# Score products of two attentions: a 64-row operand becomes a zero-padded 128-row one

## The chip, the cores and the metric

The kernel runs on one core of one Trainium2 chip. The metric is the device time of one execution in microseconds (us); several runs are taken and their median is compared. Engines are named as the profile names them: PE is TensorE's matmul, PEld its weight load, DVE VectorE, ACT ScalarE, POOL GpSimd, SP SyncE.

## The reference, cut to what matters

Two layers of a transformer over 256 context and 256 latent tokens: a feed-forward half step, a token mixer, a second feed-forward half step, and a last norm. The token mixer runs three branches (an mLSTM scan, differential attention, neighbourhood attention), gates them and merges them through `w_branch` and `w_out`. The change concerns the scores of the two attentions, which have heads of 64 features:

```python
    # differential attention: 4 heads, each with two score maps
    s1 = (jnp.einsum('bhqd,bhkd->bhqk', q1, k1) * scale).astype(jnp.float32)
    s2 = (jnp.einsum('bhqd,bhkd->bhqk', q2, k2) * scale).astype(jnp.float32)
    p = jax.nn.softmax(s1, axis=-1) - lam * jax.nn.softmax(s2, axis=-1)
...
    # neighbourhood attention: 8 heads; latent keys carry a bias, context keys none
    s_lat = (jnp.einsum('bnqhd,bknwhd->bnhqkw', qb, kb) * scale).astype(jnp.float32) + bias
    s_ctx = (jnp.einsum('bnqhd,bchd->bnhqc', qb, kc) * scale).astype(jnp.float32)
```

In the first layer context queries (which see context keys alone) are worked out too; in the last layer only latent queries.

## The kernel before, in words

**Arithmetic.** Matrices are multiplied in float32 by splitting each number into a part with its leading 11 bits (`hi`) and the rest (`lo`), and adding up hi x hi, hi x lo and lo x hi. `three` (L228) issues these three products for one block of 128 x 128 weights against all tokens of a slice (512 columns in the first layer, 256 or 512 in the last); `dense` (L234) runs `three` over the blocks and calls `tick` after each. Weights are loaded by SP into a ring `raw`, split into `whi` on ACT (L217) and `wlo` on DVE (L218).

**Scores.** `halves` (L905) takes a projection with two heads of 64 features on the 128 partitions (in PSUM) and builds tiles of 128 rows. For queries, tile j holds head j's leading part on its own 64 partitions and its rest on the other 64. For keys, tile j holds head j's leading part twice; one further tile `rest` holds the rest of both heads, each on its own 64 partitions. `qk_scores` (L918) then issues two products per head and query tile of 128: L920 multiplies the queries' leading part with the keys' rest, over the head's own 64 rows; L921 multiplies the whole query tile with the doubled keys, over all 128 rows. The query tile is the operand that is loaded as weights, the keys (512 columns, or 256 for context queries) stream. Both add up in one PSUM bank.

```python
            own = slice(64 * j, 64 * j + 64)
            mm(pS[:, 0:nk], q[j][own, bb], k[2][own, 0:nk], start=True, stop=False)
            mm(pS[:, 0:nk], q[j][:, bb], k[j][:, 0:nk], start=False, stop=True)
```

**Who calls it.** `df_head` (L954) and `na_pair` (L1032) each work on two heads (j = 0 and 1) per query tile, so four score products come in a row. Each is a generator of three stages per query tile, run by `piped` (L943): `scores` (products, then maximum on DVE, exponential on ACT, normalising on DVE), `turned` (transposes on PE at L652, copied out by ACT) and `read` (products with the values, L991 and L1073). There are four calls of `df_head` and four of `na_pair` in each of two layers. `df_qk` (L933) and `na_qk` (L1024) make the tiles for the next one.

**Order of work.** PE's order is the program's order; the tile framework orders the other engines by priority and sets all semaphores. The dense products of `merge` (gates, the next head's projections, the branch product) run as the main stream, and `Beside` lets a generator make a step after given ticks: `spread` with the lists `AT_FULL` (first layer) and `AT_LAT` (last). So the score products of one head stand between dense products of other work.

**Buffers.** Nearly all tiles of the mixer of 128 x 512 words come from one ring with the tag `t2k` of `TB` = 17 places: gate vectors, convolutions, decay weights, query and key tiles, exponentials, transposed exponentials, biases. `mt2` (L767), read by the mLSTM heads at L833, has a room of its own. POOL does few things here: a power in `pow_rstd` (L646), the loads of the neighbourhood bias (`na_bias`, L1017) which it issues itself, and small memsets.

Of the kernel before, what the change touches and what calls it, by code (L numbers as in the profile page):

```python
# [10 lines left out]
F32 = mybir.dt.float32  # L11
F32R = mybir.dt.float32r
# [4 lines left out]
P = 128  # L17
# [7 lines left out]
T = NCTX + NLAT  # L25
# [10 lines left out]
TB = 17  # L36
# [18 lines left out]
class Beside:  # L55
    """Work for the gaps of a stream of dense products: steps of generators, spread over its ticks."""
# [7 lines left out]
    def at(self, gen, ticks):  # L64
        """Steps of a generator after that many ticks from now."""
        self.timed.append([gen, [self.count + t for t in ticks]])
# [25 lines left out]
class Joined:  # L92
    """[P, n, T] in two tiles, the second from the place m: its room serves another tile before."""
# [18 lines left out]
def tile_backbone(ctx: ExitStack, tc: tile.TileContext, I, out: bass.AP):  # L112
# [36 lines left out]
    # silu(c), in 32 columns of which the first two are tokens  # L149
# [7 lines left out]
    def ada_first(l, mod, part, room):  # L157
        """Half of one of the nine vectors, as products, a step per 256 rows of w_ada."""
        pa = psum()
        c0 = mod * D + part * 512  # L160
        for k2 in range(KC // 2):
            raw = room[:, k2, :]
            nc.sync.dma_start(out=raw.rearrange("p (k c) -> p k c", k=2),
                              in_=I["w_ada0"][k2 * 256:(k2 + 1) * 256, c0:c0 + 512].rearrange("(k p) c -> p k c", k=2))
            for k in range(2):
                kc = 2 * k2 + k
                for j in range(4):
                    mm(pa[32 * j:32 * j + 32, 0:P], sc[:, kc, :], raw[:, k * 512 + j * P:k * 512 + (j + 1) * P],
                       start=kc == 0, stop=kc == KC - 1)
            yield  # L170
        rows = np_.tile([P, 256], F32, tag="rows", name="rows", bufs=1)[:, 0:P]
        with tc.high_priority(offset=AHEAD):
            nc.scalar.copy(rows, pa[:, 0:P])
        yield
        pt = psum()
        nc.tensor.transpose(pt[:, 0:P], rows, ident)
        ks = slice(4 * part, 4 * part + 4)
        v = pt[:, 0:P].rearrange("p (j c) -> p j c", j=4)
        with tc.high_priority(offset=AHEAD):
            for cls in range(2):  # L180
                nc.vector.tensor_tensor(modT[l][:, mod, cls, ks], v[:, :, cls], b_ada[:, l, mod, ks], ALU.add)
                if mod % 3 == 1:
                    nc.vector.scalar_tensor_tensor(amod[l][:, mod // 3, cls, ks], modT[l][:, mod, cls, ks], 1.0,
                                                   norm_g[:, l, mod // 3, ks], ALU.add, ALU.mult)

    def ada(l, mod, pool, scb, junk):
        """One of the nine vectors beside dense products: 64 columns of w_ada on each half of the
        partitions, of one half of its rows each, times silu(c) and added up along the rows."""
        acc = pool.tile([P, KC, 2, 2], F32, tag="acc", name="acc", bufs=2)
        for kc in range(KC):  # L190
            raw = wp.tile([P, 1024], F32, tag="raw", name="raw", bufs=4)
            nc.sync.dma_start(out=raw, in_=I["w_adaT"][l, mod, kc])
            for i in range(2):
                w = raw[:, i * 512:(i + 1) * 512]
                for cls in range(2):
                    nc.vector.scalar_tensor_tensor(w if cls else junk, w, 1.0, scb[:, cls, :], ALU.mult, ALU.mult,  # L196
                                                   accum_out=acc[:, kc, i, cls:cls + 1])
            yield
        other = pool.tile([P, KC, 2], F32, tag="other", name="other", bufs=2)
        for i in range(2):  # L200
            own, far = slice(64 * i, 64 * i + 64), slice(64 - 64 * i, 128 - 64 * i)
            nc.scalar.copy(other[own], acc[far, :, i, :])
            nc.vector.tensor_tensor(other[own], other[own], acc[own, :, i, :], ALU.add)
        for cls in range(2):
            nc.vector.tensor_tensor(modT[l][:, mod, cls, :], other[:, :, cls], b_ada[:, l, mod, :], ALU.add)
        which, what = divmod(mod, 3)
        if what == 1:
            for cls in range(2):
                nc.vector.scalar_tensor_tensor(amod[l][:, which, cls, :], modT[l][:, mod, cls, :], 1.0,
                                               norm_g[:, l, which, :], ALU.add, ALU.mult)  # L210
        elif what == 2:
            nc.vector.tensor_scalar_mul(gmod[l][:, which], modT[l][:, mod], 0.5 if which == 1 else 0.25)
        yield

    def split(hi, lo, src):
        """The leading 11 bits of float32 numbers, and the rest."""
# [11 lines left out]
    def three(dst, w, wat, a, aat, start, stop):  # L228
        """dst (+)= w.T @ a in float32, of parts with 11 bits: the weights stay."""
# [4 lines left out]
    def dense(pt, w, k0, a, at, first, last, n=KC):  # L234
        """n blocks of 128 rows of the weights, the k0-th of the product first."""
# [19 lines left out]
    def rstd_cols(cs):  # L255
        """1 / rms of the tokens of cs, on partitions, a column per 128 of them."""
# [10 lines left out]
    def rstd_rows(cs):  # L267
        """1 / rms of the tokens of cs, on every partition, in PSUM."""
# [21 lines left out]
    def norm_mod(l, which, h, cls):  # L290
        """h of one class of tokens; steps with a wait between them."""
# [18 lines left out]
    def norm_begin(l, which, h, before):  # L310
        """h of the context tokens, beside the last products of the sub-layer in front, which are
        of latent tokens; then the steps that lead to h of those."""
# [18 lines left out]
    def load_late():  # L331
        """Constants that later parts read: behind the first weights."""
# [38 lines left out]
    def ffn(l, i, classes, out_classes_next, before, vectors):  # L371
        """`before` is the end of the sub-layer in front: its last products of latent tokens."""
# [28 lines left out]
        def cold_start(n):  # L401
            """The first n units of the kernel. Shift and scale of its first norm come in halves."""
# [47 lines left out]
        def warm_start():  # L450
            """The first pair of tiles, of the scaled x alone, while the rest of the norm is worked out:
            1 / rms multiplies their products, and the products of the shift are added."""
# [20 lines left out]
            # the row 32 * g for g, a part of a unit of weights  # L473
# [25 lines left out]
        elif both:  # L499
            # two pairs of tiles take the context first, while the norm of the latent tokens runs  # L500
# [40 lines left out]
        def whole(dt):  # L541
# [5 lines left out]
            if not both:  # L547
                # what the last norm takes, with its weights, in the place of the context tokens
# [34 lines left out]
    def mixers(l, before):  # L583
# [64 lines left out]
        def transposed(tiles):  # L648
            """Blocks [128, 128] side by side, each transposed, in PSUM."""
# [55 lines left out]
        # -- mLSTM: gates and values --  # L705
# [61 lines left out]
        mt2 = mp.tile([P, T], F32R, name="mt2")  # L767
# [8 lines left out]
        # [token, tile, (g fwd, g bwd, m fwd, m bwd), head]  # L776
# [31 lines left out]
        # query tiles that a key tile reaches, per direction  # L808
# [92 lines left out]
        # -- differential attention --  # L901
# [3 lines left out]
        def halves(pt, cs, key):  # L905
            """Two heads of 64 features in parts of 11 bits, one tile of 128 rows per head: of
            queries both parts, of keys the leading part twice; and the rest of the keys."""
            two = [t2r("st") for _ in range(2)]
            rest = t2r("rest") if key else None
            for j, t in enumerate(two):  # L910
                own, other = slice(64 * j, 64 * j + 64), slice(64 - 64 * j, 128 - 64 * j)
                nc.scalar.copy(t[own, cs], pt[own, cs])
                if key:
                    nc.scalar.copy(t[other, cs], pt[own, cs])
                nc.vector.tensor_sub((rest[own, cs] if key else t[other, cs]), pt[own, cs], t[own, cs].bitcast(F32))
            return two + [rest] if key else two

        def qk_scores(pS, q, k, j, bb, nk):  # L918
            own = slice(64 * j, 64 * j + 64)
            mm(pS[:, 0:nk], q[j][own, bb], k[2][own, 0:nk], start=True, stop=False)  # L920
            mm(pS[:, 0:nk], q[j][:, bb], k[j][:, 0:nk], start=False, stop=True)  # L921

        def rope(pt):
            """Latent tokens of a projection turned, in place."""
# [18 lines left out]
        def piped(stages, items):  # L943
            """Item n is in stage s at step n + s; a wait after every piece."""
# [61 lines left out]
        # -- neighbourhood attention --  # L1006
        relb = I["relb"]

        def na_bias(b, hp2):
            """8 * bias + mask of two heads for the query tile b: [query, head, key row, key column]."""  # L1010
# [72 lines left out]
        # -- the order of work: products, with the attention of the head in front beside them --  # L1083
# [60 lines left out]
        def ended(dt, pt):  # L1144
            for cls in (0, 1) if full else (1,):
                residual(l, 1, dt, pt, cls, True)
            if not full:
                # what the next norm scales, without 1 / rms, in the place of the context tokens
# [39 lines left out]
    # the last norm: tokens to partitions while 1 / rms is worked out  # L1188
# [52 lines left out]
def _layout(i):  # L1241
    """Arrays as the chip reads them: moved, padded with zeros, never computed with."""
# [18 lines left out]
    def blocks(w, n):  # L1261
        """[.., K, n * 128] -> [.., n, 128, K]: per column block, its rows' 128 x 128 blocks side by side."""
# [61 lines left out]
```

## Time and profile before

| | us |
|---|---|
| median of 3 runs | 2328.62 |
| lowest and highest | 2328.49, 2329.36 |
| span of the profiled execution, first to last instruction | 2327.4 |
| PE busy (share of the span) | 2294.7 (99%) |
| DVE busy | 1583.6 (68%) |
| ACT busy | 936.7 (40%) |
| POOL busy | 63.3 (3%) |

The page gives the profiled execution by its span; the median of the runs is 1.2 us longer, which is what lies around the span. PE's busy share is the share of time in which some product is between its start and its modelled end; since products are pipelined, the distance from one start to the next tells more than the duration of one.

### The profile page before, as it was taken

The page shows a single profiled execution, that of the slowest core. Times are in us where ns is not written, and L with a number is a line of the kernel's source. Part 1 is how long each engine was busy: PE and PEld are TensorE (multiplying, and loading weights), DVE is VectorE, ACT ScalarE, POOL GpSimd, SP SyncE. Part 2 cuts the span into 40 slices and gives each one's busy share as a digit, 9 for nine tenths or more (in the row PEclk, how much of TensorE's full clock was granted, in tenths as well). Part 3 has the DMA queues.
Part 4 walks back from the last instruction along what each step waited for, and adds up shares of the span by engine and source line. Part 5 has one row for each costly group of instructions (what it writes and reads, how often), then busy time and mean ns, then how long its engine had stood idle before and what let it go on. Part 6 is the DMA issues. An engine that isn't in the chain of part 4 may idle for free.

```text
span 2327.4 us, 33611 instructions
## 1 busy us (share of the span) xinstructions
PE 2294.7 (99%) x12877; PEld 1952.4 (84%) x12877; DVE 1583.6 (68%) x3394; ACT 936.7 (40%) x1683; POOL 63.3 (3%) x101
## 2 busy tenths in 40 slices
PE   7999999999999999999999999999999999999998
PEld 5888889888777777888888898888898988899998
DVE  5989934786665553676666569998347875768654
ACT  4332222455544443333322233322234665555443
POOL 0000000000001100000000000000000001100000
PEclk9999999999999999999999999999999999999999
DMA  8555633212123322334444436555333233445554
GB/s 297 181 199 199 206 114 97 102 61 73 65 74 88 82 77 77 109 109 158 150 161 141 141 103 206 206 202 192 92 96 109 89 121 115 121 140 170 185 179 134
DMA packets 94257, 315.54 MB, mean 136 GB/s; under 512 B 13152, under 2 KB 13936, under 8 KB 94096
## 3 DMA queue, kind: packets, MB, share of 16 engines
q1 hardware_dynamic: 89072, 308.07, 39.1%
q0 software_dynamic: 2144, 4.36, 1.4%
q8 instruction: 101, 1.65, 0.3%
q10 hardware_dynamic: 2880, 0.96, 0.2%
q14 instruction: 60, 0.49, 0.1%
HBM read 312.30 MB, written 1.05 MB: 135 GB/s over the span
## 4 chain that ended last, share of the span: by engine, by line
PE 96%; DVE 1%; DMA 1%; ACT 1%; issue 1%; SPq 0%; POOLq 0%; POOL 0%; DVEq 0%; ACTq 0%
PE p L230 27%; PE p L232 27%; PE p L231 27%; PE p L627 2%; PE p L629 2%; PE p L628 2%; PE p L921 2%; PE p L920 2%; PE p L652 1%; PE p L868 1%; PE p L1073 1%; DMA room<-in_w_ada 1%; PE p L991 1%; PE p L845 1%; DVE wlo L218 0%
## 5 line engine op out<-in xcount | busy, mean ns | idle before, releaser
L230 PE MATMUL p<-hlo,whi 128*128 128x512 f32 (+1 forms) x2456 | 872.8, 355 | 3.5 <-DVE hlo L287 3.4
L232 PE MATMUL p<-hhi,wlo 128*128 128x512 f32 (+1 forms) x2456 | 857.0, 349 | 0.0
L231 PE MATMUL p<-hhi,whi 128*128 128x512 f32 (+1 forms) x2456 | 857.0, 349 | 0.0
L217 ACT CAST whi<-raw 128x1024 fp32r<-128x1024 f32 (+1 forms) x438 | 453.3, 1035 | 913.0 <-PE p L231 805.8
L218 DVE TENSOR_TENSOR wlo<-raw,whi 128x1024 fp32r<-128x1024 f32 (+1 forms) x438 | 526.2, 1202 | 309.2 <-ACT whi L217 308.2
L230 PEld LDWEIGHTS p<-hlo,whi 128*128 128x128 f32 x2456 | 465.3, 189 | 64.0 <-DVE hlo L287 4.1
L232 PEld LDWEIGHTS p<-hhi,wlo 128*128 128x128 f32 x2456 | 465.1, 189 | 60.4
L231 PEld LDWEIGHTS p<-hhi,whi 128*128 128x128 f32 x2456 | 465.4, 189 | 58.7 <-issue 1.9
L232 PE MATMUL p<-ghi,wlo 128*128 128x256 f32 (+1 forms) x836 | 278.2, 333 | 0.0
L231 PE MATMUL p<-ghi,whi 128*128 128x256 f32 (+1 forms) x836 | 276.8, 331 | 0.0
L196 DVE SCALAR_TENSOR_TENSOR junk<-raw,scb 128x512 f32<-128x512 f32 x256 | 175.8, 687 | 88.8 <-DMA raw<-in_w_adaT 88.5
L230 PE MATMUL p<-glo,whi 128*128 128x256 f32 (+1 forms) x616 | 203.1, 330 | 1.2 <-DVE x L305 1.2
L196 DVE SCALAR_TENSOR_TENSOR raw<-raw,scb 128x512 f32<-128x512 f32 x256 | 176.5, 689 | 6.1
L232 PEld LDWEIGHTS p<-ghi,wlo 128*128 128x128 f32 x836 | 156.9, 188 | 17.4
L231 PEld LDWEIGHTS p<-ghi,whi 128*128 128x128 f32 x836 | 156.8, 188 | 16.8
L230 PEld LDWEIGHTS p<-glo,whi 128*128 128x128 f32 x616 | 115.8, 188 | 11.5 <-DVE x L305 1.6
L305 DVE SCALAR_TENSOR_TENSOR x<-p,gmod,x 128x256 f32<-128x256 f32 x80 | 36.5, 480 | 86.1 <-PE p L232 85.8
L627 PE MATMUL p<-wlo,hhi 128*128 128x512 f32 x192 | 76.1, 396 | 0.0
L629 PE MATMUL p<-whi,hlo 128*128 128x512 f32 x192 | 74.9, 390 | 0.0
L628 PE MATMUL p<-whi,hhi 128*128 128x512 f32 x192 | 74.8, 389 | 0.0
L217 ACT CAST ghi<-g 128x512 fp32r<-128x512 f32 (+1 forms) x88 | 49.9, 567 | 46.4 <-DVE g L392 46.0
L230 PE MATMUL p<-olo,whi 128*128 128x512 f32 (+1 forms) x192 | 68.3, 356 | 0.0
(232 smaller groups left out, 2363.8 us busy)
## 6 DMA issues: line engine op xcount, KB each, us to landing
raw<-in_w SPq DMA_DIRECT2D x208, 512.0 KB, 3.3
raw<-in_w_adaT SPq DMA_DIRECT2D x128, 512.0 KB, 3.3
raw<-in_wf SPq DMA_DIRECT2D x106, 512.0 KB, 3.2
raw<-in_w SPq DMA_DIRECT2D x64, 448.0 KB, 3.3
raw<-in_wv SPq DMA_DIRECT2D x24, 512.0 KB, 3.2
raw<-in_wb SPq DMA_DIRECT2D x24, 512.0 KB, 3.2
room<-in_w_ada SPq DMA_DIRECT2D x16, 512.0 KB, 10.0
raw<-in_wo SPq DMA_DIRECT2D x16, 512.0 KB, 3.2
```

Of the source, the lines that this page charges most:

```text
L196: nc.vector.scalar_tensor_tensor(w if cls else junk, w, 1.0, scb[:, cls, :], ALU.mult, ALU.mult, accum_out=acc[:, kc, i, cls:cls + 1])
L217: nc.scalar.copy(hi, src)
L218: nc.vector.tensor_sub(lo, src, hi.bitcast(F32))
L230: mm(dst, w[0][:, wat], a[1][:, aat[0], aat[1]], start=start, stop=False)
L231: mm(dst, w[0][:, wat], a[0][:, aat[0], aat[1]], start=False, stop=False)
L232: mm(dst, w[1][:, wat], a[0][:, aat[0], aat[1]], start=False, stop=stop)
L305: nc.vector.scalar_tensor_tensor(x[:, dt, cs], pt[:, cs], gmod[l][:, which, cls, dt:dt + 1], x[:, dt, cs], ALU.mult, ALU.add)
L627: mm(pts[t], h[0][:, kc, at], w[1][:, wat], start=kc == 0, stop=False)
L628: mm(pts[t], h[0][:, kc, at], w[0][:, wat], start=False, stop=False)
L629: mm(pts[t], h[1][:, kc, at], w[0][:, wat], start=False, stop=kc == KC - 1)
L920: mm(pS[:, 0:nk], q[j][own, bb], k[2][own, 0:nk], start=True, stop=False)
L921: mm(pS[:, 0:nk], q[j][:, bb], k[j][:, 0:nk], start=False, stop=True)
```

## The change

`halves` makes one tile per head for the rest of the keys, with the head's rest on its own 64 partitions and zeros on the other 64; the zeros are written by a memset on POOL. `qk_scores` multiplies the whole query tile with it, over 128 rows. The ring `t2k` has 19 places, and `mt2` takes one of them in place of its own room. (Comments that the diff deletes are left out here.)

```diff
-TB = 17
+TB = 19
...
-        mt2 = mp.tile([P, T], F32R, name="mt2")
+        mt2 = mp.tile([P, T], F32R, tag="t2k", name="mt2", bufs=TB)
...
             two = [t2r("st") for _ in range(2)]
-            rest = t2r("rest") if key else None
+            rests = [t2r("rest") for _ in range(2)] if key else []
             for j, t in enumerate(two):
                 own, other = slice(64 * j, 64 * j + 64), slice(64 - 64 * j, 128 - 64 * j)
+                if key:
+                    nc.gpsimd.memset(rests[j][other, cs].bitcast(F32), 0.0)
                 nc.scalar.copy(t[own, cs], pt[own, cs])
                 if key:
                     nc.scalar.copy(t[other, cs], pt[own, cs])
-                nc.vector.tensor_sub((rest[own, cs] if key else t[other, cs]), pt[own, cs], t[own, cs].bitcast(F32))
-            return two + [rest] if key else two
+                nc.vector.tensor_sub((rests[j][own, cs] if key else t[other, cs]), pt[own, cs], t[own, cs].bitcast(F32))
+            return two + rests
 
         def qk_scores(pS, q, k, j, bb, nk):
-            own = slice(64 * j, 64 * j + 64)
-            mm(pS[:, 0:nk], q[j][own, bb], k[2][own, 0:nk], start=True, stop=False)
+            mm(pS[:, 0:nk], q[j][:, bb], k[2 + j][:, 0:nk], start=True, stop=False)
             mm(pS[:, 0:nk], q[j][:, bb], k[j][:, 0:nk], start=False, stop=True)
```

## Rows read from the trace of the kernel before

**Rows 1.** The page: busy time by engine, and the chain that ended last.

```profile
PE 2294.7 (99%) x12877; PEld 1952.4 (84%) x12877; DVE 1583.6 (68%) x3394; ACT 936.7 (40%) x1683; POOL 63.3 (3%) x101
...
PE 96%; DVE 1%; DMA 1%; ACT 1%; issue 1%; SPq 0%; POOLq 0%; POOL 0%; DVEq 0%; ACTq 0%
```

**Rows 2.** Line L920: its instructions (duration ns min/median/max, first and last start us, forms).

```profile
L920 PE MATMUL p<-rest,st x96: 377/492/502, 566.3 to 2060.5; 64*128 64x512 f32 x64, 64*128 64x256 f32 x32
L920 PEldq EVENT_SEMAPHORE  x16: 51/51/51, 598.6 to 2053.8; - x16
```

**Rows 3.** Timeline of PE, four products of 512 columns (start us, us, what).

```profile
582.67 0.39 PE L231 MATMUL p<-hhi,whi 128*128 128x512 f32 x1
582.90 0.40 PE L232 MATMUL p<-hhi,wlo 128*128 128x512 f32 x1
583.23 0.50 PE L920 MATMUL p<-rest,st 64*128 64x512 f32 x1
583.66 0.50 PE L921 MATMUL p<-st 128*128 128x512 f32 x1
...
584.51 0.50 PE L921 MATMUL p<-st 128*128 128x512 f32 x1
584.85 0.39 PE L230 MATMUL p<-hlo,whi 128*128 128x512 f32 x1
...
586.68 0.39 PE L232 MATMUL p<-hhi,wlo 128*128 128x512 f32 x1
```

**Rows 4.** Timeline of PEld over the same stretch.

```profile
582.68 0.19 PEld L232 LDWEIGHTS p<-hhi,wlo 128*128 128x128 f32 x1
583.23 0.18 PEld L920 LDWEIGHTS p<-rest,st 64*128 64x128 f32 x1 [0.36 <-issue]
583.66 0.19 PEld L921 LDWEIGHTS p<-st 128*128 128x128 f32 x1 [0.25 <-issue]
...
584.62 0.19 PEld L230 LDWEIGHTS p<-hlo,whi 128*128 128x128 f32 x1
```

**Rows 5.** Timeline of PE, four products of 256 columns.

```profile
566.03 0.39 PE L232 MATMUL p<-hhi,wlo 128*128 128x512 f32 x1
566.34 0.38 PE L920 MATMUL p<-rest,st 64*128 64x256 f32 x1
...
567.28 0.39 PE L921 MATMUL p<-st 128*128 128x256 f32 x1
567.50 0.39 PE L230 MATMUL p<-hlo,whi 128*128 128x512 f32 x1
```

**Rows 6.** Timeline of PE, dense products of 256 columns in the last layer.

```profile
1931.79 0.28 PE L230 MATMUL p<-hlo,whi 128*128 128x256 f32 x1
...
1932.51 0.28 PE L230 MATMUL p<-hlo,whi 128*128 128x256 f32 x1
```

**Rows 7.** POOL by line and shape: xcount, busy us, mean ns, idle before us.

```profile
L151 POOL MEMSET sc<- 128x256 f32 x1 | 0.3, 341 | 0.0
...
L641 POOL MEMSET v<- 128x64 f32 x2 | 0.3, 152 | 16.3 <-ACT hhi L286 16.3
```

**Rows 8.** Timeline of POOL: the bias loads of the second pair.

```profile
758.73 4.95 POOL L1017 DMA_DIRECT2D braw<-in_relb  x8 [33.48 <-PE p L921]
```

**Rows 9.** Timeline of all engines: keys of one head made, and first used.

```profile
635.78 0.69 DVE L915 TENSOR_TENSOR rest<-p,st 64x512 fp32r<-64x512 f32 x1 [1.25 <-ACT st L914]
...
638.30 0.38 PE L920 MATMUL p<-rest,st 64*128 64x256 f32 x1
```

**Rows 10.** PE by line and shape: the transposes of exponentials.

```profile
L652 PE MATMUL p<-c_ident,ne 128*128 128x128 f32 x160 | 21.8, 273 | 1.7 <-DVE nsm L1052 0.8 <-DVE nmx L1048 0.5 <-ACT nT L1063 0.4
...
L652 PE MATMUL p<-c_ident,de 128*128 128x128 f32 x80 | 12.7, 272 | 0.6 <-DVE de L976 0.6
```

**Rows 11.** Window of one differential head, last layer: busy by engine, PEclk, DMA share, GB/s.

```profile
1867.00:1890.00 23.00, 23.00 (x154) 20.09 (x153) 17.33 (x37) 16.34 (x35) 0.00 (x0) 1.00 0.34 120
```

**Rows 12.** Line L833: the products that read `mt2`.

```profile
L833 PE MATMUL p<-mt,nselr x16: 279/338/400, 462.7 to 1833.4; 128*128 128x512 f32 x8, 128*128 128x256 f32 x8
```

## The prediction

> **What bounds the kernel now.** I read the page first. PE is busy for 99% of the span, and the chain that ended last consists of PE for 96%, so what is saved in PE's order of work is saved in the end, as long as nothing else comes late [rows 1]. DVE and ACT have room over the whole span, and POOL does nearly nothing [rows 1].
>
> A busy PE is not a fast PE, since a product counts as busy from its start to its modelled end. So I read next the line of the 64-row products, then the timeline of PE around one set of four score products, and took distances between starts. Eight dense products of 512 columns follow each other from 584.85 to 586.68 us, 0.229 us apiece [rows 3]. The four score products are not like that: the dense product in front of them holds PE for 0.33 us (582.90 to 583.23), the first 64-row product for 0.43, and the last 128-row product for 0.34 [rows 3].
>
> The timeline of weight loads tells why. The load of dense L232 starts at 582.68, together with the product of L231 in front of it, and is hidden there; the load of L230 behind the set starts at 584.62, inside the last score product [rows 4]. But the load of a 64-row product, and that of the 128-row product behind it, start only when their own product does, after 0.36 and 0.25 us without a load [rows 4]. So the cost sits where a product of 64 rows and one of 128 rows are neighbours, in either order; between two products of 128 rows, score or dense, there is none. The last score product separates the two parts of it: its own load was not hidden, its successor's was, and it takes 0.34, so a load standing alone costs 0.11; the others take 0.43, so the change of height costs 0.09 more.
>
> **The change, part by part.**
>
> *The 64-row product gets 128 rows.* All four products then have the height of the dense ones, and I take the dense distance for each. A set of 512 columns lasts 1.95 us now, counted from the start of the dense product before it to the start of the one behind it (582.90 to 584.85); five dense distances are 1.15, so 0.80 goes. A set of 256 columns lasts 1.47 (566.03 to 567.50) [rows 5]. Dense products of 256 columns start every 0.12 us (0.72 for six) [rows 6], so 0.23 and four times 0.12 make 0.71, and 0.76 goes. There are 96 first products, 64 of 512 and 32 of 256 columns [rows 2], two to a set: 32 x 0.80 + 16 x 0.76 = 37.8 us. The shapes hardly vary over the kernel: the durations run from 377 to 502 ns, which are the two widths [rows 2]. Rounding leaves 1 us either way.
>
> The height itself is free by the same rows: dense products use all 128 rows at 0.229 us for 512 columns, close to a column per cycle at 2.4 GHz, and the granted clock is 1.00 in the attention stage [rows 11]. The zero rows add nothing to the sums.
>
> What the Trainium skill says against this stands in "TensorE: Matmul & The Clock Gate", Part 3, "The mechanism": a weight load overlaps a running product only where their row groups differ. By that rule the padded products, which share all rows with their neighbours, would keep their loads in the open, and the saving would be the changes of height alone. The trace does not agree, since dense loads of 128 rows lie inside dense products of 128 rows [rows 4]; as a rival it is priced below.
>
> *The memsets.* Sixteen sets of keys (four per attention and layer), two memsets each, 64 x 512 words. POOL's memsets took 0.152 us for 64 words a partition and 0.341 for 256 [rows 7], so 0.98 ns a word and 0.59 us for 512: 32 x 0.59 = 19 us on an engine that is busy for 3% [rows 1]. They read nothing, so they wait only for a place in the ring. The bounds are 0 and 19 us. I take 0: the differential heads' memsets find POOL idle, and a memset can run while ACT and DVE still make the other parts; at the tightest place that I found DVE's last part starts at 635.78 and PE reads it at 638.30, still 1.8 us after its end [rows 9]. In neighbourhood attention a memset may have to stand behind the bias loads of the next pair, which wait 33 us for the last scores of the pair before and then hold POOL for 4.95 us [rows 8]. That is what queues behind a waiting POOL instruction, and the other way round the bias loads would queue behind a memset. The loads there end at 763.7 us, and by the order of the program a branch product and a gate projection lie between the keys that they would delay by 1.2 us and the first scores.
>
> *The waits of PE.* The first product of a set of keys now waits for POOL too. PE's queue has 16 separate wait instructions on L920, one per set of keys, of 51 ns each [rows 2]. One more for each is 16 x 0.051 = 0.8 us; bounds 0 and twice that. I take 0.8.
>
> *DVE, ACT and softmax.* The copies and subtractions keep number and size. What changes is when they must be done: PE reaches the transposes sooner. They already wait for 1.7 us in neighbourhood attention and 0.6 us in differential attention, in all [rows 10]. The first head's maximum can start when the second product ends, 0.69 us before the dense product behind the set (584.16 to 584.85) [rows 3]. With dense distances it has three of them less the duration of a product, 0.69 - 0.39 = 0.30. So 0.4 us of lead goes per set. Behind the fourth product nothing changes. Where transposes wait already, at some four places, up to 1.6 us comes back; if every set lost it, 48 x 0.4 = 19. I take 1.0, near the lower end, as waits are rare in 240 transposes [rows 10]. Throughput does not bind: in the fullest attention stage that I looked at, a differential head of the last layer, DVE is busy for 17.3 of 23 us and ACT for 16.3 [rows 11]. Taking two sets' 1.6 us from that window leaves DVE at 81%.
>
> *The ring.* Two heads' tiles can be alive at once. Before, that is ten query and key tiles of 17 places; after, twelve of 19: seven are left for exponentials and biases in both. In the mLSTM stage `mt2` holds one of 19, so 18 are left against 17. `mt2` is written while PE runs the value products and read from 462.7 us to 1833.4 [rows 12], and it is free again before the first score product of its layer. Nothing is taken for this edit; the bound is the slower rival below.
>
> **Sum.** 37.8 - 0.8 - 1.0 = 36.0 us off the profiled execution's 2327.4, so 2291.4. The runs' median is 1.2 us longer than that span: 2328.6 - 36.0 = **2292.6 us**. With every cost at nothing and the rounding on the good side it is 2289.8. With half of the 19 us of lost lead coming back it is about 2301.
>
> **The rivals.**
>
> 1. *Slower: the ring runs short.* The framework hands out places by priority, and a memset without inputs can take its place early, when another tile needs it. Then an exponential waits until an older one has been read, and PE stands before the transposes. If that costs each set two steps of the main stream (three dense products, 0.69 us, each), it is 48 x 1.4 = 67 us against 36: 2360 us. It decides from 0.75 us per set. For it: the bias loads already wait 33 us for places that score products free [rows 8]. Against it: the count of seven free places is kept. 4%.
>
> 2. *Memsets or softmax come late.* The 19 us of memsets lie half open, or the lead is lost everywhere: 9 to 19 us of the gain go back, 2302 to 2312. Against it stand POOL's 3% and the 1.8 us in hand [rows 1, 9]. 5%.
>
> 3. *The loads stay in the open.* Only the changes of height go: in a set of 512 columns 0.10 in front and three times 0.09, that is 0.37, so 48 x 0.37 = 18 us: 2311. That is what the rule named above would give. Against it: every dense product [rows 4]. 3%.
>
> 4. *The height is not the cause.* The extra time could belong to something else about these operands, such as the tiles that ACT and DVE write in parts; then nothing is saved, 0.8 us is added, and it is 2329. Against it: the 128-row score product pays the change only with a 64-row neighbour; followed by a dense product it pays the load alone [rows 3, 4]. 3%.
>
> **How the numbers follow.** The forecast has 85%, and its own range is 2289 to 2301. Widened to the near end of the second rival, 2302, at least 8 in 10 are held. Faster by over 0.2% (4.7 us, about what a measurement of this kernel can tell from no change) are the forecast and rivals 2 and 3: 93%. Rival 4 is no change, 3%; rival 1 is slower, 4%.
>
> **What would show it.** In the profile after: L920 with 128 x 128 weights and a duration near 390 ns for 512 columns where it was 500; both score lines starting 0.23 us apart (0.12 for 256); loads of L920 and L921 inside the product before. POOL has 32 more memsets of about 0.6 us, none of which is named as what ended a wait of PE. Sets of 512 columns last 1.15 us. It is wrong if starts stay 0.34 us apart (rival 3) or 0.43 (rival 4), if PE's idle time before L920 names POOL (rival 2), or if its idle time before L652 grows by far more than 2 us (rivals 1 and 2).

## The result, and the profile after

The changed kernel takes 2292.0 us in the median of four runs (2290.1 to 2294.2) against 2328.9: a ratio of 0.984 with a 95% interval of 0.9826 to 0.9854, so 34 to 41 us less. The prediction was 2292.6.

The profiled execution is the shortest of the four, with a span of 2288.3 us. On its page, the busy times by engine (to be read beside [rows 1]):

```profile
PE 2256.8 (99%) x12877; PEld 1951.1 (85%) x12877; DVE 1582.0 (69%) x3394; ACT 936.1 (41%) x1683; POOL 79.6 (3%) x133
```

PE has as many products as before and is busy for 37.9 us less. DVE and ACT do the same work. POOL has 32 more instructions and 16.3 us more work. PE is still what bounds the kernel.

The score line of the changed kernel, which is L922 now (duration ns min/median/max, first and last start us, forms; the answer to [rows 2]):

```profile
L922 PE MATMUL p<-rest,st x96: 278/388/397, 565.6 to 2021.8; 128*128 128x512 f32 x64, 128*128 128x256 f32 x32
L922 PEldq EVENT_SEMAPHORE  x32: 51/51/51, 561.6 to 2016.4; - x32
```

The products have the height of the dense ones and their durations, and PE's queue has twice as many separate waits. The timeline of PE around a set of 512 columns (start us, us, what; [rows 3]):

```profile
579.89 0.40 PE L232 MATMUL p<-hhi,wlo 128*128 128x512 f32 x1
580.13 0.39 PE L922 MATMUL p<-rest,st 128*128 128x512 f32 x1
580.36 0.39 PE L923 MATMUL p<-st 128*128 128x512 f32 x1
580.58 0.39 PE L922 MATMUL p<-rest,st 128*128 128x512 f32 x1
580.81 0.40 PE L923 MATMUL p<-st 128*128 128x512 f32 x1
581.05 0.39 PE L230 MATMUL p<-hlo,whi 128*128 128x512 f32 x1
```

Every start follows the one before it by 0.22 to 0.24 us, and the set lasts 1.16 us where it lasted 1.95. The first set of 256 columns, on PE ([rows 5]):

```profile
565.41 0.40 PE L232 MATMUL p<-hhi,wlo 128*128 128x512 f32 x1
565.65 0.28 PE L922 MATMUL p<-rest,st 128*128 128x256 f32 x1
...
566.00 0.28 PE L923 MATMUL p<-st 128*128 128x256 f32 x1
566.12 0.39 PE L230 MATMUL p<-hlo,whi 128*128 128x512 f32 x1
```

and the weight loads of the same set ([rows 4]):

```profile
565.42 0.19 PEld L922 LDWEIGHTS p<-rest,st 128*128 128x128 f32 x1
565.65 0.19 PEld L923 LDWEIGHTS p<-st 128*128 128x128 f32 x1
...
566.00 0.19 PEld L230 LDWEIGHTS p<-hlo,whi 128*128 128x128 f32 x1
```

It lasts 0.71 us where it lasted 1.47. The load of the first score product (565.42) starts with the dense product in front of it (565.41), and that of the second with the first: no load stands alone any more.

What the change adds shows on POOL (by line and shape: xcount, busy us, mean ns, idle before us and what ended it):

```profile
L1019 POOL DMA_DIRECT2D braw<-in_relb x64 | 39.3, 630 | 2.4 <-DVE p L1047 1.1 <-issue 1.0
L914 POOL MEMSET rest<- 64x512 f32 x32 | 16.7, 523 | 460.6 <-PE p L868 210.1 <-PE p L1075 85.4 <-PE p L652 46.2
```

A memset takes 0.52 us. The memsets wait for places in the ring, 461 us in all, and the bias loads behind them hardly wait any longer; before, it was the bias loads that waited for score products [rows 8].

One reading trap is on this page. The chain that ended last names PE for 87% and "issue" for 9%, where it had been PE for 96% [rows 1]. The chain in order of time shows that the 9% is one piece:

```profile
PE 87%; issue 9%; DVE 2%; ACT 1%; DMA 1%; SPq 0%; POOL 0%; POOLq 0%; DVEq 0%; ACTq 0%
...
2090.58 190.81 issue
```

It lies in front of the last norm, where the walk back goes through POOL's power and then into POOL's own idle time, while PE works. It is no cost that the change brought: the power of that norm stands behind the same idle time in both kernels (the timelines of POOL, before and after):

```profile
2320.54 0.70 POOL L264 TENSOR_TENSOR r<-r,half 128x2 f32<-128x2 f32 x1 [190.85 <-DVE r L263]
2281.43 0.70 POOL L264 TENSOR_TENSOR r<-r,half 128x2 f32<-128x2 f32 x1 [190.85 <-DVE r L263]
```

Nor do the shares go with the time. The pages of experiment 2, which takes the time of the kernel before, and of experiment 1, which takes that of the changed one, have

```profile
PE 88%; issue 9%; DVE 2%; DMA 1%; ACT 1%; POOL 0%; SPq 0%; POOLq 0%; DVEq 0%; ACTq 0%
PE 96%; DVE 2%; DMA 1%; ACT 1%; issue 1%; SPq 0%; POOLq 0%; POOL 0%; DVEq 0%; ACTq 0%
```

The 9% is in all five profiles of kernels with the memsets (the changed kernel and experiments 2, 4, 5 and 7) and in none of the five without (the kernel before and experiments 1, 3, 6 and 8). Why the walk goes that way with them is not shown.

### The profile page after: what moved, and what is told of

Its sections match the earlier page's. It is cut to its first block, busy times and chain, and to the rows that moved or that the text cites. A ratio compares the mean times of both kernels' runs of the same rounds, so it can differ in the third digit from the quotient of the medians.

```text
span 2288.3 us, 33698 instructions
## 1 busy us (share of the span) xinstructions
PE 2256.8 (99%) x12877; PEld 1951.1 (85%) x12877; DVE 1582.0 (69%) x3394; ACT 936.1 (41%) x1683; POOL 79.6 (3%) x133
## 4 chain that ended last, share of the span: by engine, by line
PE 87%; issue 9%; DVE 2%; ACT 1%; DMA 1%; SPq 0%; POOL 0%; POOLq 0%; DVEq 0%; ACTq 0%
PE p L230 25%; PE p L232 25%; PE p L231 25%; PE p L627 2%; PE p L629 2%; PE p L628 2%; PE p L652 1%; PE p L868 1%; PE p L1075 1%; DMA room<-in_w_ada 1%; PE p L923 1%; PE p L922 1%; PE p L993 1%; PE p L845 1%; DVE wlo L218 0%
```

## The experiments

All times stand beside runs of the kernel before on the same chip: 2328.8 us for the first four, 2329.0 us for the last four.

**1. The height alone.** The kernel before, with the first product over all 128 rows of the one shared `rest` tile. There the other 64 rows hold the other head's rest in place of zeros.

```diff
-            own = slice(64 * j, 64 * j + 64)
-            mm(pS[:, 0:nk], q[j][own, bb], k[2][own, 0:nk], start=True, stop=False)
+            mm(pS[:, 0:nk], q[j][:, bb], k[2][:, 0:nk], start=True, stop=False)
```

> The kernel before, with one line changed: the first score product takes all 128 rows of the query tile and of the one shared rest tile. No memset, no second tile, ring of 17 and mt2 as before. It adds one stray term to each score, the queries' rest times the other head's keys' rest (both below the leading 11 bits). Height theory: all of the gain comes from the one line; sets of 512 columns last 1.15 us, sets of 256 last 0.71, time 2290 to 2293 us. If the gain came from the ring of 19 places or from mt2's room: 2329 us. If the operand's making (tiles written in parts by ACT and DVE) were the cause: 2329 us.

2290.65 us (five runs, 2290.3 to 2293.4), ratio 0.9838 (0.9824 to 0.9851). The whole gain is there without memset, second tile or ring. The line of its first score product, which is L919 here (columns as above), and a set of 512 columns on PE, which lasts 1.16 us:

```profile
L919 PE MATMUL p<-rest,st x96: 278/388/397, 565.5 to 2021.9; 128*128 128x512 f32 x64, 128*128 128x256 f32 x32
L919 PEldq EVENT_SEMAPHORE  x7: 51/51/51, 629.4 to 1902.3; - x7
```

```profile
579.75 0.40 PE L232 MATMUL p<-hhi,wlo 128*128 128x512 f32 x1
579.99 0.39 PE L919 MATMUL p<-rest,st 128*128 128x512 f32 x1
...
580.67 0.40 PE L920 MATMUL p<-st 128*128 128x512 f32 x1
580.91 0.39 PE L230 MATMUL p<-hlo,whi 128*128 128x512 f32 x1
```

**2. The new buffers with the old height.** The kernel after, with 64 rows again.

```diff
-            mm(pS[:, 0:nk], q[j][:, bb], k[2 + j][:, 0:nk], start=True, stop=False)
+            own = slice(64 * j, 64 * j + 64)
+            mm(pS[:, 0:nk], q[j][own, bb], k[2 + j][own, 0:nk], start=True, stop=False)
```

> The kernel after, with the first score product back at 64 rows; the two zero-padded tiles, the 32 memsets, the ring of 19 and mt2 in it stay. Height theory: nothing is gained, the sets last 1.95 us (512) and 1.47 us (256) again, time 2328 to 2330 us. Ring theory (the gain comes from buffers): 2292 us. If memsets or the extra waits cost anything, it lies above the kernel before by that: up to 0.8 us for the waits, up to 19 us for the memsets.

2328.54 us, ratio 0.9998 (0.9989 to 1.0007): buffers gain nothing and cost nothing that can be seen. Its score line, and its memsets on POOL:

```profile
L923 PE MATMUL p<-rest,st x96: 377/492/502, 566.1 to 2060.2; 64*128 64x512 f32 x64, 64*128 64x256 f32 x32
```

```profile
L914 POOL MEMSET rest<- 64x512 f32 x32 | 16.6, 520 | 481.3 <-PE p L868 210.0 <-ACT nT L1066 63.5 <-PE p L652 51.1
```

The durations are those of [rows 2] to the nanosecond in the extremes, although the operands now come from the padded tiles. Experiments 1 and 2 together leave the height as the only cause: each differs from a kernel with the other time by nothing but the rows of this one product.

**3. Fewer changes of height.** The kernel before, with the products of a set in another order.

```diff
-        def qk_scores(pS, q, k, j, bb, nk):
-            own = slice(64 * j, 64 * j + 64)
-            mm(pS[:, 0:nk], q[j][own, bb], k[2][own, 0:nk], start=True, stop=False)
-            mm(pS[:, 0:nk], q[j][:, bb], k[j][:, 0:nk], start=False, stop=True)
+        def qk_scores(pSs, q, k, bb, nk):
+            for j in range(2):
+                own = slice(64 * j, 64 * j + 64)
+                mm(pSs[j][:, 0:nk], q[j][own, bb], k[2][own, 0:nk], start=True, stop=False)
+            for j in range(2):
+                mm(pSs[j][:, 0:nk], q[j][:, bb], k[j][:, 0:nk], start=False, stop=True)
...
-                for j in range(2):
-                    qk_scores(pSs[j], q, k, j, bb, nk)
+                qk_scores(pSs, q, k, bb, nk)
```

> The kernel before, with the four products of a set in another order: both 64-row products first, then both 128-row ones. Nothing else changes. Height theory: a set has two changes of height in place of four. Dense product in front 0.33, first 64-row product 0.34 (its load in the open), second 64-row product 0.32 (load hidden, then the change), first 128-row product 0.34, last 0.23: 1.56 us for 512 columns against 1.96, 0.4 us less per set, 48 x 0.4 = 19 us, so 2310 us. If the two 64-row products, which lie on different halves of the rows, also run side by side, another 0.23 us per set of 512 and 0.12 per set of 256 goes, 9 us: 2300 us. If the height is not the cause: 2329 us. If loads only hide behind products on other rows, the second 64-row load hides and the 128-row loads do not: 2310 us as well, but the last score product stays at 0.34 us.

2300.68 us, ratio 0.9877 (0.9864 to 0.9891): 28 us less, which is the case with two changes and the 64-row products side by side. Its timeline of PE (the two products of a line are merged):

```profile
581.51 0.39 PE L232 MATMUL p<-hhi,wlo 128*128 128x512 f32 x1
581.83 0.50 PE L921 MATMUL p<-rest,st 64*128 64x512 f32 x2
582.26 0.73 PE L923 MATMUL p<-st 128*128 128x512 f32 x2
582.83 0.39 PE L230 MATMUL p<-hlo,whi 128*128 128x512 f32 x1
```

and its weight loads:

```profile
581.82 0.19 PEld L921 LDWEIGHTS p<-rest,st 64*128 64x128 f32 x2 [0.35 <-issue]
582.25 0.30 PEld L923 LDWEIGHTS p<-st 128*128 128x128 f32 x2 [0.24 <-issue]
582.60 0.19 PEld L230 LDWEIGHTS p<-hlo,whi 128*128 128x128 f32 x1
```

The two 64-row products occupy 0.50 us from the first's start to the second's end, which is what one alone took [rows 3]: the first starts at 581.83, and the next line follows 0.43 us later. Where the trace's records are taken one by one, the second 64-row product starts 0.003 us after the first (median of the sets of 512 columns). Loads stand alone only at the two changes. The two 128-row products take 0.57 us, one distance of 0.34 and one of 0.23, and the load of the second starts 0.10 us after the first product, inside it (a narrower window, which does not merge the two loads):

```profile
582.36 0.19 PEld L923 LDWEIGHTS p<-st 128*128 128x128 f32 x1
```

So that load is hidden behind a product on the same rows. The set lasts 1.32 us; two changes less are worth 0.4 us, and the second 64-row product that costs nothing 0.23.

**4. One attention alone.** The kernel after, with 64 rows kept in neighbourhood attention.

```diff
-        def qk_scores(pS, q, k, j, bb, nk):
-            mm(pS[:, 0:nk], q[j][:, bb], k[2 + j][:, 0:nk], start=True, stop=False)
+        def qk_scores(pS, q, k, j, bb, nk, half=False):
+            own = slice(64 * j, 64 * j + 64) if half else slice(0, P)
+            mm(pS[:, 0:nk], q[j][own, bb], k[2 + j][own, 0:nk], start=True, stop=False)
...
-                    qk_scores(pSs[j], q, k, j, bb, nk)
+                    qk_scores(pSs[j], q, k, j, bb, nk, True)
```

> The kernel after, with 64 rows kept in neighbourhood attention alone (its tiles, memsets and waits stay). Height theory: the gain is by sets, and differential attention has 24 of the 48 (16 of 512 columns, 8 of 256): 16 x 0.80 + 8 x 0.76 = 18.9 us, so 2310 us. If part of the gain came from neighbourhood attention starting its bias loads or softmax sooner, differential attention would have less than half: above 2312 us.

2310.69 us, ratio 0.992 (0.9907 to 0.9934): 18 us less for half of the sets. The gain goes by the number of sets. Its score line holds both kinds:

```profile
L923 PE MATMUL p<-rest,st x96: 278/392/502, 566.8 to 2042.2; 128*128 128x512 f32 x32, 64*128 64x512 f32 x32, 128*128 128x256 f32 x16, 64*128 64x256 f32 x16
```

**5 and 6. With and without what the change adds.** The kernel after, unchanged, and the kernel of experiment 1 once more, on the same chip.

> The kernel after, unchanged, to stand beside the next one on the same chip. 2290 to 2294 us. Its runs spread over 4 us where those of the kernel before spread over 1; if that belongs to the kernel and not to the day, the spread comes again.

> The kernel before with the one changed line (128 rows of the shared rest tile; a stray term of rest times rest is added to each score), beside the kernel after. If memsets, 16 more waits and the ring cost something, this one is faster by it: the prediction took 0.8 us for the waits. If they are covered, the two agree within their spread.

2290.59 us (2289.5 to 2293.5) and 2290.89 us (2290.7 to 2291.7), both with a ratio of 0.9837 (0.9822 to 0.9851). Memsets, second tile and more waits cost nothing that shows. The waits differ by more than the expectation names: PE's queue has 32 on the first score line of the changed kernel and 7 in the kernel of experiment 6, as in experiment 1, so 25 more. Why the one-line form has fewer than the 16 of the kernel before is not shown. The spread of 4 us came again in experiment 5 (1.1 us in experiment 6), but it cannot be put down to the changed kernel: beside these, thirteen runs of the kernel before spread over 3 us, from 2327.3 to 2330.4.

**7. Four times the memsets.**

```diff
-                    nc.gpsimd.memset(rests[j][other, cs].bitcast(F32), 0.0)
+                    for _ in range(4):
+                        nc.gpsimd.memset(rests[j][other, cs].bitcast(F32), 0.0)
```

> The kernel after, with each of the 32 memsets issued four times: 96 more, 0.52 us each, 50 us more on POOL, 1.6 us more for each tile. If memsets lie beside other work: no change, 2290 to 2294 us. If they are on the path for even a quarter of their time: 12 us more, 2304 us.

2290.90 us, ratio 0.9835 (0.9819 to 0.9852): no change. The memsets on POOL (line L915 here):

```profile
L915 POOL MEMSET rest<- x128: 516/521/819, 519.0 to 2005.0; 64x512 f32 x128
```

A tile's zeros may come 1.6 us later without PE noticing. The profile is of the longest of these runs (2293.9 us), and its 48 sets last 46.5 us together, as in the profile of the changed kernel, which is of a run of 2290.1; the 4 us between them do not lie in the score products.

**8. A lower product still.** The kernel before, with 32 rows in place of 64.

```diff
-            own = slice(64 * j, 64 * j + 64)
+            own = slice(64 * j, 64 * j + 32)
```

> The kernel before, with the first score product over the first 32 of the head's 64 rows: half of the queries' leading part times the keys' rest is left out. If the cost is that of a change of height, it does not depend on how many rows the lower product has: distances of 0.43 and 0.34 us as before, 2328 to 2330 us. If time went with rows, the product would be shorter and the kernel would lie under 2325 us.

2327.93 us, ratio 0.9996 (0.9986 to 1.0007). A set on PE:

```profile
582.50 0.39 PE L232 MATMUL p<-hhi,wlo 128*128 128x512 f32 x1
582.82 0.50 PE L920 MATMUL p<-rest,st 32*128 32x512 f32 x1
...
584.10 0.50 PE L921 MATMUL p<-st 128*128 128x512 f32 x1
584.44 0.39 PE L230 MATMUL p<-hlo,whi 128*128 128x512 f32 x1
```

It lasts 1.94 us as with 64 rows. What costs is that the height differs from the neighbour's, not how low it is (64 and 32 rows were tried).

No version beat the changed kernel. The one of experiment 1 equals it with less in it, at the price of the stray term.

## Why the prediction was right

**The main term.** The step was 0.80 us for a set of 512 columns and 0.76 for one of 256, 37.8 us in all, read from distances between starts. Measured on the timelines shown, they are 1.95 - 1.16 = 0.79 and 1.47 - 0.71 = 0.76. PE's busy time fell by 37.9 us. Summed over all 48 sets of the trace, from the start of the product in front to the start of the one behind, they took 84.0 us before and take 46.5 now: 37.5 less. That the loads of padded products would be hidden like dense ones was the step with the least support, since no score product showed it; the loads of the profile after do. Rival 3 would have given 2311 us. It is what follows from the rule of the Trainium skill that a load overlaps only with products on other rows ("TensorE: Matmul & The Clock Gate", Part 3, "The mechanism"). Neither the changed kernel nor experiment 3 agrees with it: in both, loads hide behind products on the same rows. Of the 0.20 us that each change costs, 0.11 is the load that stands alone, and the timelines put 0.09 at the change itself. Another sentence of the Trainium skill, on the modes that differ in rows or columns, names such a cost: "Mode switching requires drain" ("TensorEngine Tiling (Array Packing)", "Tiling Modes"). Experiments 1, 2, 3 and 8 agree with it in that each change costs time; that it is a drain no run shows, and the page gives no price.

**Rival 4**, that the height is not the cause, fell with experiments 1 and 2.

**The memsets** were taken at nothing and cost nothing. One was 0.52 us where 0.59 was worked out. The prediction had them wait for nothing but a place in the ring, and they do, but for long: POOL stands idle for 461 us in front of them, behind mLSTM reads, transposes and value products among others. It named two orders for neighbourhood attention, memsets behind bias loads or bias loads behind memsets. The second is what came, and the loads' wait passed to the memsets. Experiment 7 shows how much room is left.

**The waits of PE** were taken at 0.8 us. The 16 more instructions are there, as named. That they wait for the zeros fits experiment 2, where the products leave the zeros out and 16 remain. But they cost nothing that shows: experiments 5 and 6, which differ by 25 such waits, differ by 0.3 us, the other way round. The first wait of the changed kernel runs at 561.6 us and the product that it guards starts at 565.6, so it lies 4 us ahead in PE's queue.

**Softmax** was taken at 1.0 us. The waits of transposes are (by line and shape, [rows 10]):

```profile
L652 PE MATMUL p<-c_ident,ne 128*128 128x128 f32 x160 | 21.8, 273 | 1.6 <-DVE nsm L1054 0.8 <-DVE nmx L1050 0.4 <-ACT nT L1065 0.4
L652 PE MATMUL p<-c_ident,de 128*128 128x128 f32 x80 | 12.7, 272 | 0.6 <-DVE de L978 0.6
```

They were 2.3 us and are 2.2: nothing came back. I read that as the case of the prediction in which a transpose hangs on the fourth product of a set, whose lead does not change; that was not tried by itself.

**Rival 2**, late memsets or softmax, has by these three nothing left to stand on: PE's wait before L652 did not grow, and PE does not wait before L922 at all, for POOL or another (by line and shape, the last figure is the idle time):

```profile
L922 PE MATMUL p<-rest,st 128*128 128x512 f32 x64 | 25.0, 391 | 0.0
L922 PE MATMUL p<-rest,st 128*128 128x256 f32 x32 | 8.2, 278 | 0.0
```

**Rival 1**, the ring, did not come. The count of seven free places in attention is not shown by any row, but with 19 places and the old height the time is that of the kernel before (experiment 2).

So the two small costs, 1.8 us together, do not show in the runs, and 37.8 us is nearer to the truth than 36.0. The later medians of the changed kernel and of its one-line form (2290.6 to 2290.9 in experiments 1, 5 and 6) are 38 us under the kernel before; the first four runs gave 36.8, with an interval (34 to 41) that holds both. The mechanism was right; that the forecast came within 0.6 us of the first median is in part luck.

## What to carry to other kernels

Between full-height products, a product over fewer rows costs more than a full one: here 0.2 us at each change, of which 0.11 is the next load standing alone and 0.09 passes at the change itself. The price does not go with the columns: four changes cost 0.79 us in a set of 512 columns and 0.76 in one of 256. Fill the rows with zeros, or with something that is harmless (38 us here), or group the low products on different rows, which then run side by side (28 us here, as two changes are left in each set). Low products on the same rows, one behind the other, were not run. Read distances between starts and the start of each load against the product before it; busy shares showed 99% before and after.

## What the runs showed that was not expected

The prediction had nothing on two 64-row products side by side. On different halves of the rows they take 0.43 us for the pair until the next product starts, the same as one alone (experiment 3); the expectation there gave it as the lower of two times, 2300 us, and the run came to 2300.7. Nor did it say what a lower product would do. The cost of a change of height does not depend on the height, as experiment 8 expected: a set lasted 1.94 us with 32 rows and 1.95 with 64.

Not expected anywhere was that the shares of the chain that ended last would go with 32 memsets that cost nothing: "issue" has 9% of it in every kernel that has them, at either time.
